# Matrix products that read their moving operand as runs of 128 columns: a decoder block in float32r on one core

## The chip, the core and the metric

The program runs on one core of a Trainium2 chip. The core has five engines with instruction queues of their own: TensorE (PE, matrix products; its weight loads have a row of their own, PEld), VectorE (DVE), ScalarE (ACT), GpSimd (POOL) and SyncE (SP, which issues most of the loads). They share an on-chip memory (SBUF) of 128 partitions; matrix products land in the accumulation memory (PSUM), in banks of 512 float32 columns.

The metric is the time of one execution on the device, in microseconds. Before the change it is 1596.77 us (median of 3 runs, 1596.67 to 1596.89).

## The reference

One layer of a decoder block over 256 tokens with 16 learned tokens put in front, width 2048. A token mixer with two branches (softmax attention with a forget gate, 8 heads; chunked gated linear attention, 4 heads) and a squared-ReLU MLP of width 8192, each after an RMS norm. All inputs are float32.

```python
def hybrid_mixer(xn, w_in, ...):
    proj = xn @ w_in                                   # 2048 x 13336
    (fq, fk, fv, ff, gq, gk, gv, gr, ga, gate_fox, gate_gla) = split(proj)
    o_fox = forgetting_attention(fq, fk, fv, ff, b_forget)
    o_gla = gated_linear_attention(gq, gk, gv, g_log)
    o_gla = head_rmsnorm(o_gla, gla_norm_g) * silu(gr)
    y = sigmoid(gate_fox) * (o_fox @ w_o_fox) + sigmoid(gate_gla) * (o_gla @ w_o_gla)
    return y @ w_out

h = concat([meta_tokens, x])
h = h + hybrid_mixer(rmsnorm(h, norm_mix_g), ...)
h = h + square(relu(rmsnorm(h, norm_mlp_g) @ w1)) @ w2
return rmsnorm(h, final_norm_g)[16:]
```

## The kernel before

Activations are kept transposed: 128 channels on the partitions, tokens along the row. Every operand of a product is held as two float32r numbers, a high part (the value cast to float32r) and a low part (what the cast left over), so that a product of two float32 matrices is made of three float32r products: high x high, high x low and low x high.

Weights come from `w_all` in chunks of 2048 input channels x 128 output channels, in the order in which they are used (`stream()`). `next_weights` loads a chunk in two halves (L118, SP), casts each to its high part on ACT (L120) and subtracts on DVE for the low part (L121). Weight halves rotate through five buffers.

The product that fills most of the program is `gemm2` (L140 ff.): for each of 16 channel blocks k it calls `mac2`, which issues two products into one bank `ps`. The first (L136) has the high weights as its stationary operand and reads 512 columns: the 256 tokens of the high part and then the 256 of the low part of the moving operand, `x[:, k]`. The second (L137) has the low weights and reads the 256 columns of the high part alone. ACT and DVE then add the two halves of the bank (`total`, L168 and L171, or `add_residual`, L858 to L860). Products over all 272 tokens (`gemm_all`, L153 to L155) come three to a block, each 272 columns wide.

The moving operands are these tiles. `x`, the normalised input, lies in the tile `x_row` (tag s1), whose row for one k has 544 words: 272 of the high part and 272 of the low part; `gemm2` reads the 512 from word 16 on. The other five come from the helper `operand` (L218 ff.): `og` (output of the linear attention, tag s2), `of` (output of the softmax attention, 8 blocks), `y` (gated sum, tag s1), `x2` (input of the MLP, tag s2) and `a` (hidden layer of the MLP, tag s1, made anew for each of four groups). It gives each k a row of 544 words too, of which 16 at each end are left unused, and hands out a view `[128, k, o, t]`: o = 0 is the high part, o = 1 the low part, t the 256 tokens. The 512 columns of one k are then one run of consecutive words, and the 256 of the high part are one run too. The rows are written by ACT (high part) and DVE (low part), mostly in `split_to` (L175, L176); `x2` by L865 and L866.

The order of the program: a first stage in which seven chunks are worked on together (L345 to L352), the four heads of linear attention, the eight of softmax attention, the gates and the two branch projections (operands `x`, `of`, `og`), the output projection (`y`), and four groups of the MLP, each 16 chunks with the operand `x2` and 16 with `a`. The last four output chunks are taken apart: their low-weight products come first (L912, 256 columns, one run) and their high-weight products then run once for each half of the tokens (L928). There the 256 columns are 128 of the high part and the same 128 tokens of the low part, so two runs of 128 with 128 words between them. Their high weights are kept in the tile `whi_last` (tag s2).

A tile framework places the instructions in the engines' queues and adds the semaphores. Nothing in the code around the change sets the order by hand, apart from the last stage.

Of the kernel before, what the change touches and what calls it, by code (L numbers as in the profile page):

```python
# [16 lines left out]
P = 128  # L17
# [48 lines left out]
def trunk(ctx: ExitStack, tc: tile.TileContext, hT, w_small, w_all, consts, w_alpha2, out):  # L66
# [3 lines left out]
    def nm(s):  # L70
        serial[0] += 1
        return f"{s}_{serial[0]}"
# [145 lines left out]
    def operand(pool, name, nk=KT, at=0, **kw):  # L218


        row = 2 * NT + 32
        t = pool.tile([P, at + nk * row], F32R, name=nm(name), **kw)
        t = t[:, at:].rearrange("p (k r) -> p k r", r=row)
        return t[:, :, 16 : 16 + 2 * NT].rearrange("p k (o t) -> p k o t", t=NT)

# [28 lines left out]
    def gain(i, k):  # L254
        return h[:, k, NA + i : NA + i + 1]
# [202 lines left out]
    def og_tile():  # L458
        if not og_box:
            og_box.append(operand(keep, "og", tag="s2"))  # L460
        return og_box[0]
# [32 lines left out]
    def gla_head(hd, sg, ready=None):  # L494
# [129 lines left out]
        def scale():  # L624
            for i in range(4):
                j = 4 * hd + i
                nc.vector.scalar_tensor_tensor(oT[:, i, :], oT[:, i, :], ggn[:, j : j + 1], rg, op0=ALU.mult,
                                               op1=ALU.mult)
                nc.vector.tensor_tensor(oT[:, i, :], oT[:, i, :], st["sg"][:, i, :], op=ALU.mult)
                split_to(og_tile()[:, j, 0, :], og_tile()[:, j, 1, :], oT[:, i, :])  # L630

# [52 lines left out]
    late = branches.enter_context(tc.tile_pool(name="late", bufs=1, reuse_waits="tile"))  # L684
    of = operand(late, "of", FOX_H, 32)
    negc = late.tile([P, FOX_H, NA], F32, name="negc")
# [18 lines left out]
    def fox_head(hd):  # L705
# [71 lines left out]
        def out_v():  # L777
            po = bank(px, "pof")
            three(po[:, 0:NT], va, pa, True, False)
            nc.tensor.matmul(po[:, P:NT], vb, pT, start=False, stop=True)  # L780
            nc.scalar.copy(of[:, hd, 0, :], po[:, 0:NT])
            nc.vector.tensor_tensor(of[:, hd, 1, :], po[:, 0:NT], of[:, hd, 0, :].bitcast(F32),
                                    op=ALU.subtract)
            nc.scalar.copy(og4[:, four], corners(po[:, 0:NT]))
# [11 lines left out]
        def fill_corners(pu, vz, pz):  # L796
            nc.tensor.matmul(pu[:, 2 * P : 3 * P], vz, pz, start=True, stop=True)
            nc.vector.tensor_tensor(og4, og4, pu[:, 2 * P : 3 * P].rearrange("p (h c q) -> p h c q", c=2, q=NM),
                                    op=ALU.add)
            hi, lo = (of[:, hd - 3 : hd + 1, o, :].rearrange("p h (c q) -> p h c q", q=P)[:, :, :, P - NM :]  # L800
                      for o in range(2))
            split_to(hi, lo, og4)

# [22 lines left out]
    for j0 in range(0, KT, 2):  # L826
# [18 lines left out]
    ht = h[:, :, NM:NA]  # L845
    x2 = operand(keep, "x2", tag="s2")

# [15 lines left out]
    for j in range(KT):  # L863
        add_residual(j, gemm2(next_weights(), y))
        nc.scalar.activation(x2[:, j, 0, :], ht[:, j, :], AF.Identity, scale=gain(1, j))  # L865
        nc.vector.scalar_tensor_tensor(x2[:, j, 1, :], ht[:, j, :], gain(1, j),  # L866
                                       x2[:, j, 0, :].bitcast(F32), op0=ALU.mult, op1=ALU.subtract)
        square_sum(j, acc2)
# [36 lines left out]

    whi = keep.tile([P, NL, KT, P], F32R, tag="s2", name="whi_last")
    ends = []
    for n in range(NL):
        j, ps = KT - NL + n, bank(pg if n < 3 else px, "ps")
        w = next_weights(whi[:, n])  # L910
        for k in range(KT):
            nc.tensor.matmul(ps[:, 0:NT], w(k)[1], a[:, k, 0, :], start=(k == 0), stop=(k == KT - 1))  # L912
        nc.vector.tensor_tensor(ht[:, j, :], ps[:, 0:NT], ht[:, j, :], op=ALU.add)
        ends.append((j, w, ps))

    def half(t0, between, within=None):
# [4 lines left out]
        for n, (j, w, ps) in enumerate(ends):  # L921
            for k in range(KT):
                if within and n == NL - 1 and k == 4:
                    ahead = within()
                elif not (within and n == NL - 1 and k > 4):
                    ahead = None
                with tc.issue_after(ahead) if ahead else nullcontext():
                    nc.tensor.matmul(ps[:, NT:], w(k)[0], a[:, k, :, tok], start=(k == 0), stop=(k == KT - 1))  # L928
            between[n]()
# [129 lines left out]
```

## Time and profile before

| | |
|---|---|
| median of 3 runs | 1596.77 us (1596.67 to 1596.89) |
| profiled execution, span from the first to the last instruction | 1595.0 us |
| PE busy | 1585.0 us, 99% |
| PEld busy | 1428.8 us, 90% |
| DVE busy | 1060.4 us, 66% |
| ACT busy | 790.8 us, 50% |
| POOL busy | 125.2 us, 8% |
| granted TensorE clock, mean | 0.998 |
| HBM over the span | 183 GB/s |

The span leaves out what lies before the first and after the last instruction; the runs are longer than it by 1596.77 - 1595.0 = 1.8 us. Matrix products are pipelined: the duration of one in a row of the profile is longer than the time from its start to the start of the next, so the cost of one is read from start to start. In the groups by line the profile leaves out numbers in names, so `x` there stands for `x` and `x2` together.

### The profile page before, as it was taken

The page shows a single profiled execution, that of the slowest core. Times are in us where ns is not written, and L with a number is a line of the kernel's source. Part 1 is how long each engine was busy: PE and PEld are TensorE (multiplying, and loading weights), DVE is VectorE, ACT ScalarE, POOL GpSimd, SP SyncE. Part 2 cuts the span into 40 slices and gives each one's busy share as a digit, 9 for nine tenths or more (in the row PEclk, how much of TensorE's full clock was granted, in tenths as well). Part 3 has the DMA queues.
Part 4 walks back from the last instruction along what each step waited for, and adds up shares of the span by engine and source line. Part 5 has one row for each costly group of instructions (what it writes and reads, how often), then busy time and mean ns, then how long its engine had stood idle before and what let it go on. Part 6 is the DMA issues. An engine that isn't in the chain of part 4 may idle for free.

```text
span 1595.0 us, 25427 instructions
## 1 busy us (share of the span) xinstructions
PE 1585.0 (99%) x9812; PEld 1428.8 (90%) x9812; DVE 1060.4 (66%) x1659; ACT 790.8 (50%) x1271; POOL 125.2 (8%) x213
## 2 busy tenths in 40 slices
PE   9999999999999999999999999999999999999997
PEld 8999999999998888888888888888888888888887
DVE  7897757676655555555777776567655776567655
ACT  6665444454455444444555544444444444444563
POOL 6011000011100000000011000000000000000022
PEclk9999999999999999999999999999999999999999
DMA  9444545454445555555555555555555555555552
GB/s 323 156 164 155 180 157 183 167 188 164 159 167 181 191 186 189 189 191 187 186 195 186 188 193 187 188 191 190 187 190 190 186 189 193 186 188 193 186 183 97
DMA packets 86602, 293.09 MB, mean 184 GB/s; under 512 B 9112, under 2 KB 16800, under 8 KB 86352
## 3 DMA queue, kind: packets, MB, share of 16 engines
q1 hardware_dynamic: 85872, 289.62, 53.8%
q8 instruction: 77, 1.26, 0.3%
q0 software_dynamic: 176, 1.12, 0.2%
q10 hardware_dynamic: 432, 0.72, 0.1%
q14 instruction: 45, 0.37, 0.1%
HBM read 289.32 MB, written 2.11 MB: 183 GB/s over the span
## 4 chain that ended last, share of the span: by engine, by line
PE 99%; DMA 0%; issue 0%; POOL 0%; ACT 0%; DVE 0%; SPq 0%; POOLq 0%; ACTq 0%
PE ps L136 51%; PE ps L137 27%; PE psa L155 5%; PE psa L154 5%; PE psa L153 5%; PE ps L345 1%; PE ps L350 1%; PE ps L928 1%; PE pa L548 1%; PE ps L912 0%; DMA raw<-w_all_dram 0%; PE po L611 0%; POOL o L976 0%; PE po L188 0%; PE ps L348 0%
## 5 line engine op out<-in xcount | busy, mean ns | idle before, releaser
L121 DVE TENSOR_TENSOR wlo<-raw,whi 128x1024 fp32r<-128x1024 f32 x522 | 641.0, 1228 | 452.8 <-ACT whi L120 449.4
L120 ACT CAST whi<-raw 128x1024 fp32r<-128x1024 f32 x522 | 548.1, 1050 | 660.0 <-PE ps L136 493.1
L136 PE MATMUL ps<-x,whi 128*128 128x512 f32 x1952 | 683.8, 393 | 0.0
L137 PE MATMUL ps<-x,wlo 128*128 128x256 f32 x1952 | 548.5, 281 | 0.0
L136 PEld LDWEIGHTS ps<-x,whi 128*128 128x128 f32 x1952 | 366.1, 188 | 80.4
L137 PEld LDWEIGHTS ps<-x,wlo 128*128 128x128 f32 x1952 | 368.3, 189 | 0.1
L136 PE MATMUL ps<-a,whi 128*128 128x512 f32 x960 | 334.3, 392 | 0.0
L137 PE MATMUL ps<-a,wlo 128*128 128x256 f32 x960 | 269.1, 281 | 0.0
L136 PEld LDWEIGHTS ps<-a,whi 128*128 128x128 f32 x960 | 179.8, 188 | 39.9
L137 PEld LDWEIGHTS ps<-a,wlo 128*128 128x128 f32 x960 | 181.1, 189 | 0.3
L153 PE MATMUL psa<-x,whi 128*128 128x272 f32 x624 | 181.2, 290 | 0.0
L155 PE MATMUL psa<-x,whi 128*128 128x272 f32 x624 | 181.1, 290 | 0.0
L154 PE MATMUL psa<-x,wlo 128*128 128x272 f32 x624 | 179.4, 288 | 0.0
L153 PEld LDWEIGHTS psa<-x,whi 128*128 128x128 f32 x624 | 118.1, 189 | 0.4
L154 PEld LDWEIGHTS psa<-x,wlo 128*128 128x128 f32 x624 | 117.4, 188 | 0.0
L155 PEld LDWEIGHTS psa<-x,whi 128*128 128x128 f32 x624 | 117.2, 188 | 0.0
L136 PE MATMUL ps<-og,whi 128*128 128x512 f32 x256 | 89.6, 392 | 0.0
L136 PE MATMUL ps<-y,whi 128*128 128x512 f32 x256 | 89.1, 392 | 0.0
L854 POOL TENSOR_TENSOR acc<-acc,hsq 128x256 f32<-128x256 f32 x26 | 28.5, 1097 | 769.2 <-ACT hsq L853 769.2
L137 PE MATMUL ps<-og,wlo 128*128 128x256 f32 x256 | 71.9, 281 | 0.0
L137 PE MATMUL ps<-y,wlo 128*128 128x256 f32 x256 | 71.8, 281 | 0.0
L171 DVE TENSOR_TENSOR evt<-ps,evb 128x256 f32<-128x256 f32 x158 | 65.9, 418 | 0.5 <-ACT evb L168 0.5
(301 smaller groups left out, 1437.0 us busy)
## 6 DMA issues: line engine op xcount, KB each, us to landing
raw<-w_all_dram SPq DMA_DIRECT2D x537, 512.0 KB, 3.6
raw<-w_all_dram SPq DMA_DIRECT2D x8, 384.0 KB, 6.6
h<-hT_dram SPq DMA_DIRECT2D x8, 275.0 KB, 6.7
negc<-fdram POOLq DMA_DIRECT2D x1, 1088.0 KB, 8.0
out_dram<-o SPq DMA_DIRECT2D x2, 512.0 KB, 2.7
raw<-w_all_dram SPq DMA_DIRECT2D x2, 256.0 KB, 3.9
room<-w_small_dram SPq DMA_DIRECT2D x1, 320.0 KB, 7.4
out_dram<-o ACTq DMA_DIRECT2D x1, 320.0 KB, 3.1
```

Of the source, the lines that this page charges most:

```text
L120: nc.scalar.copy(hi[:, k, :], r)
L121: nc.vector.tensor_tensor(lo[:, k, :], r, hi[:, k, :].bitcast(F32), op=ALU.subtract)
L136: nc.tensor.matmul(ps, hi, x, start=first, stop=False)
L137: nc.tensor.matmul(ps[:, 0:NT], lo, x[:, 0, :], start=False, stop=last)
L153: nc.tensor.matmul(ps[:, 0:NA], hi, x_hi[:, k], start=(k == 0), stop=False)
L154: nc.tensor.matmul(ps[:, 0:NA], lo, x_hi[:, k], start=False, stop=(k == KT - 1))
L155: nc.tensor.matmul(ps[:, X_LO], hi, x_lo[:, k], start=False, stop=(k == KT - 1), skip_group_check=True)
L171: nc.vector.tensor_tensor(t, ps[:, 0:NT], b, op=ALU.add)
L345: nc.tensor.matmul(ps, hi, x[:, k], start=st, stop=False)
L350: nc.tensor.matmul(ps[:, 0:NT], lo, x[:, k, 0], start=False, stop=sp)
L548: nc.tensor.matmul(dst, k[:, a], q[:, a, :], start=(a == 0), stop=(a == 1))
L854: nc.gpsimd.tensor_tensor(acc, acc, sq, op=ALU.add)
```

## The change

`operand` no longer leaves unused words between rows. A row for one k now has 512 words, split in two halves of the tokens, a = 0 and a = 1; in each half stand the 128 words of the high part and then the 128 of the low part. The view is `[128, k, o, a, t]` with t of 128. Read in the order o, a, t, the 512 columns of a product are four runs of 128 words, at words 0, 256, 128 and 384 of the row, and the 256 of the high part are two, at words 0 and 256. The order of the columns in the bank is as before. In L928 the high and low words of one half of the tokens now lie side by side, so that its 256 columns are one run.

The tile sizes stay nearly the same (`of` gets 32 words less), and the spare words serve as an offset `at` ahead of the first row: 64 for `og` and `x2`, 96 for `of` and `y`, and 96, 64, 80, 64 for the four groups of `a`. The writers address the rows as two runs of 128 (`pair`). In `fox_head` a copy and a subtraction become a call of `split_to`, which issues the same two instructions. `whi_last` begins 16 words further on. `x`, `gemm_all` and the first stage are not touched.

```diff
     def operand(pool, name, nk=KT, at=0, **kw):
-        row = 2 * NT + 32
-        t = pool.tile([P, at + nk * row], F32R, name=nm(name), **kw)
-        t = t[:, at:].rearrange("p (k r) -> p k r", r=row)
-        return t[:, :, 16 : 16 + 2 * NT].rearrange("p k (o t) -> p k o t", t=NT)
+        t = pool.tile([P, nk * (2 * NT + 32)], F32R, name=nm(name), **kw)
+        return t[:, at : at + nk * 2 * NT].rearrange("p (k a o t) -> p k o a t", a=2, o=2, t=P)
+
+    def pair(ap):
+        return ap.rearrange("p (a t) -> p a t", t=P)
...
-            og_box.append(operand(keep, "og", tag="s2"))
+            og_box.append(operand(keep, "og", at=64, tag="s2"))
...
-                split_to(og_tile()[:, j, 0, :], og_tile()[:, j, 1, :], oT[:, i, :])
+                split_to(og_tile()[:, j, 0], og_tile()[:, j, 1], pair(oT[:, i, :]))
...
-    of = operand(late, "of", FOX_H, 32)
+    of = operand(late, "of", FOX_H, 96)
...
-            nc.scalar.copy(of[:, hd, 0, :], po[:, 0:NT])
-            nc.vector.tensor_tensor(of[:, hd, 1, :], po[:, 0:NT], of[:, hd, 0, :].bitcast(F32),
-                                    op=ALU.subtract)
+            split_to(of[:, hd, 0], of[:, hd, 1], pair(po[:, 0:NT]))
...
-    y = operand(keep, "y", tag="s1")
+    y = operand(keep, "y", at=96, tag="s1")
     for j in range(KT):
-        split_to(y[:, j, 0, :], y[:, j, 1, :], yf[:, j, :])
+        split_to(y[:, j, 0], y[:, j, 1], pair(yf[:, j, :]))
...
-    x2 = operand(keep, "x2", tag="s2")
+    x2 = operand(keep, "x2", at=64, tag="s2")
...
-        nc.scalar.activation(x2[:, j, 0, :], ht[:, j, :], AF.Identity, scale=gain(1, j))
+        nc.scalar.activation(x2[:, j, 0], pair(ht[:, j, :]), AF.Identity, scale=gain(1, j))
...
-        split_to(a[:, f, 0, :], a[:, f, 1, :], s)
+        split_to(a[:, f, 0], a[:, f, 1], pair(s))
...
-        a = operand(keep, "a", tag="s1")
+        a = operand(keep, "a", at=(96, 64, 80, 64)[g], tag="s1")
...
-    whi = keep.tile([P, NL, KT, P], F32R, tag="s2", name="whi_last")
+    whi = keep.tile([P, 16 + NL * KT * P], F32R, tag="s2", name="whi_last")[:, 16:].rearrange(
+        "p (n k m) -> p n k m", k=KT, m=P)
...
-            nc.tensor.matmul(ps[:, 0:NT], w(k)[1], a[:, k, 0, :], start=(k == 0), stop=(k == KT - 1))
+            nc.tensor.matmul(ps[:, 0:NT], w(k)[1], a[:, k, 0], start=(k == 0), stop=(k == KT - 1))
...
-                    nc.tensor.matmul(ps[:, NT:], w(k)[0], a[:, k, :, tok], start=(k == 0), stop=(k == KT - 1))
+                    nc.tensor.matmul(ps[:, NT:], w(k)[0], a[:, k, :, t0 // P], start=(k == 0), stop=(k == KT - 1))
```

More of the change, by code (lines that the diff above doesn't have):

```diff
@@ L799, in fill_corners @@
                                     op=ALU.add)
-            hi, lo = (of[:, hd - 3 : hd + 1, o, :].rearrange("p h (c q) -> p h c q", q=P)[:, :, :, P - NM :]
-                      for o in range(2))
-            split_to(hi, lo, og4)
+            split_to(*(of[:, hd - 3 : hd + 1, o, :, P - NM :] for o in range(2)), og4)
         later(1, turn_v)
@@ L864, in trunk @@
         add_residual(j, gemm2(next_weights(), y))
-        nc.scalar.activation(x2[:, j, 0, :], ht[:, j, :], AF.Identity, scale=gain(1, j))
-        nc.vector.scalar_tensor_tensor(x2[:, j, 1, :], ht[:, j, :], gain(1, j),
-                                       x2[:, j, 0, :].bitcast(F32), op0=ALU.mult, op1=ALU.subtract)
+        nc.scalar.activation(x2[:, j, 0], pair(ht[:, j, :]), AF.Identity, scale=gain(1, j))
+        nc.vector.scalar_tensor_tensor(x2[:, j, 1], pair(ht[:, j, :]), gain(1, j),
+                                       x2[:, j, 0].bitcast(F32), op0=ALU.mult, op1=ALU.subtract)
         square_sum(j, acc2)
```

## The prediction

> **What bounds the kernel now.** I read the page's shares first, then the chain that ended last, then the groups by line, and last the instructions of PE in order of time.
>
> ```profile
> span 1595.0 us, 25427 instructions
> PE 1585.0 (99%) x9812; PEld 1428.8 (90%) x9812; DVE 1060.4 (66%) x1659; ACT 790.8 (50%) x1271; POOL 125.2 (8%) x213
> PEclk9999999999999999999999999999999999999999
> PE 99%; DMA 0%; issue 0%; POOL 0%; ACT 0%; DVE 0%; SPq 0%; POOLq 0%; ACTq 0%
> PE ps L136 51%; PE ps L137 27%; PE psa L155 5%; PE psa L154 5%; PE psa L153 5%; PE ps L345 1%; PE ps L350 1%; PE ps L928 1%; PE pa L548 1%; PE ps L912 0%; DMA raw<-w_all_dram 0%; PE po L611 0%; POOL o L976 0%; PE po L188 0%; PE ps L348 0%
> ...
> L136 PE MATMUL ps<-x,whi 128*128 128x512 f32 x1952 | 683.8, 393 | 0.0
> L137 PE MATMUL ps<-x,wlo 128*128 128x256 f32 x1952 | 548.5, 281 | 0.0
> L136 PE MATMUL ps<-a,whi 128*128 128x512 f32 x960 | 334.3, 392 | 0.0
> L136 PE MATMUL ps<-og,whi 128*128 128x512 f32 x256 | 89.6, 392 | 0.0
> L136 PE MATMUL ps<-y,whi 128*128 128x512 f32 x256 | 89.1, 392 | 0.0
> L136 PE MATMUL ps<-of,whi 128*128 128x512 f32 x128 | 45.1, 393 | 0.0
> ```
>
> The chain is PE for 99% of the span, and 78% of it is the two lines of `mac2`; the clock is granted in full throughout. In the groups the number behind the last bar, idle time of PE ahead of the group, is 0.0 everywhere. No semaphore holds these products up, so only their own pace counts. The mean durations (393, 281 ns) overlap; the pace is in the starts:
>
> ```profile
> 1099.76 0.39 PE L136 MATMUL ps<-x,whi 128*128 128x512 f32 x1
> 1099.99 0.28 PE L137 MATMUL ps<-x,wlo 128*128 128x256 f32 x1
> 1100.11 0.39 PE L136 MATMUL ps<-x,whi 128*128 128x512 f32 x1
> ...
> 1103.94 0.39 PE L136 MATMUL ps<-x,whi 128*128 128x512 f32 x1
> ```
>
> This is the operand `x2`. From the first to the last row shown there are 12 pairs (one L136, one L137): (1103.94 - 1099.76) / 12 = 348.3 ns a pair. The operand `a` goes at the same pace, (1002.92 - 999.79) / 9 = 347.8 ns:
>
> ```profile
> 999.79 0.39 PE L136 MATMUL ps<-a,whi 128*128 128x512 f32 x1
> ...
> 1002.92 0.39 PE L136 MATMUL ps<-a,whi 128*128 128x512 f32 x1
> ```
>
> **The change part by part.** *How many products.* The groups give 960 (`a`), 256 (`og`), 256 (`y`) and 128 (`of`) pairs; of the 1952 listed under `x`, the four MLP groups have 4 x 16 chunks x 16 blocks = 1024 with `x2`, and 928 keep the operand `x` and their one run. Changed: 2624 pairs, which now take 2624 x 348.3 ns = 914 us, 57% of the span. One nanosecond on a pair is 2.6 us. I call 0.2% (3.2 us, about what a measurement of this kernel can tell from no change) the bound of "the same"; it is 1.2 ns on a pair.
>
> *What two runs cost.* One line of the kernel before reads its 256 columns as two runs of 128 already, L928; beside it stands L912, 256 columns in one run of the same tile. The chain of the last microseconds (start, length, what) shows both with nothing between:
>
> ```profile
> 1562.51 5.68 PE ps L912 x48
> 1568.18 1.65 PE ps L928 x14
> 1569.84 0.95 PE ps L912 x8
> 1570.78 0.23 PE ps L928 x2
> 1571.02 0.94 PE ps L912 x8
> 1571.96 7.47 PE ps L928 x64
> ```
>
> One run: 5.68 / 48 = 118.3 ns. Two runs: 1.65 / 14 = 117.9 ns in the first stretch and 7.47 / 64 = 116.7 ns in the long one. A second run of 128 costs nothing that these rows show, and in the long stretch the product is 1.6 ns shorter. That is the nearest row to every product that the change touches.
>
> *L137, from one run to two* (words 0 and 256 of the row, the same step as in L928 before): 1.6 ns less by the long stretch, 0.4 by the first: 2624 x 1.6 = 4.2 us less, between 1.0 and 4.2. I take 4.2, since the long stretch is the steady one.
>
> *L136, from one run to four.* No row has four runs. With a gain for each further run it would be 3 x 1.6 = 4.8 ns, 12.6 us less. On the other side stands what a start costs: a 512-column product takes 348.3 - 118.3 = 230.0 ns, two of 256 take 236.6, so a product has some 6.6 ns that don't go with its columns (an estimate from these rows). If each of three further runs paid that, it would be 19.8 ns, 52 us more; L928 speaks against it. I take the same 1.6 ns as for two runs, once for the product: 4.2 us less.
>
> *Where the rows lie.* Rows of 544 words begin at a new place modulo 128 words with each k; rows of 512 words all begin at the same place, which `at` chooses. No row of before compares places apart from others; the 1.2 ns between the two stretches of L928, whose instruction is the same, is the size of what such things do here. I take 0; if all products of a tile sat at the better or worse end, it would be 1.2 x 2 x 2624 = 6.3 us to either side.
>
> The page "TensorE: Matmul & The Clock Gate" of the Trainium skill (section "Wait — 56ns, not 53.3ns?") has N / 2.4 GHz + 2.5 ns from start to start: 215.8 and 109.2, or 325 ns a pair, where the rows have 348.3. The trace doesn't agree, by 23 ns a pair; if the change took all of that away, an estimate by that page is 2624 x 23 ns = 60 us less, some 1536 us.
>
> *The last stage.* L928 goes from two runs to one, 128 x 1.6 = 0.2 us more; L912 from one to two, 64 x 1.6 = 0.1 less. `whi_last` moves by 16 words: 0, with both ends inside the 1.2 ns x 128 = 0.2 us of the two stretches. Together +0.1 us.
>
> *The writers.* 16 rows of `og`, 8 of `of`, 16 of `y`, 16 of `x2` and 64 of `a` are written, 120 on ACT and 120 on DVE, now as two runs:
>
> ```profile
> L176 DVE TENSOR_TENSOR a<-asq,a 128x256 fp32r<-128x256 f32 x64 | 26.6, 419 | 0.0
> L175 ACT CAST a<-asq 128x256 fp32r<-128x256 f32 x64 | 25.5, 401 | 0.0
> L121 DVE TENSOR_TENSOR wlo<-raw,whi 128x1024 fp32r<-128x1024 f32 x522 | 641.0, 1228 | 452.8 <-ACT whi L120 449.4
> L120 ACT CAST whi<-raw 128x1024 fp32r<-128x1024 f32 x522 | 548.1, 1050 | 660.0 <-PE ps L136 493.1
> ```
>
> DVE sat idle for 452.8 us ahead of L121 alone, and ACT for 660.0 ahead of L120, mostly for a free weight buffer, that is, for PE. If each write took twice as long, DVE would work 120 x 0.419 = 50 us more and ACT 48 us more, both well inside that idle time. Cost 0, covered by PE's products; were the cover gone, those 50 us would be the price. No DMA, wait or instruction is added or moved past a queue, on SP and POOL neither; the merged `split_to` issues the same two instructions.
>
> *Sum.* 1595.0 - 4.2 - 4.2 + 0.1 = 1586.7 us of span; with the 1.8 us by which the median of the runs (1596.77) exceeds it, 1588.5 us.
>
> **The rivals.** *Nothing changes.* The difference between 118.3 and 116.7 needn't be the runs: the first stretch of L928 has the same two runs and goes at 117.9. Then the pace comes from the order of loads and products, a run of 128 words is as good as one of 512, and the time stays 1596.8. For it: that first stretch. Against it: the long one, 64 products without a pause. The page "SBUF — State Buffer" of the Trainium skill (section "Specifications (TRN2)") points the same way: reads pay when they cross from one 16-byte line to the next, and runs of 128 float32 words that begin at multiples of 16 words cross as many lines as before. No run here shows that by itself.
>
> *The further runs of L136 stall the reading (slower).* L928 shows one jump inside a product of 256 columns; three jumps in 512 columns, back and forth (words 0, 256, 128, 384), may not be hidden as one is. At a quarter of a start, 1.65 ns a jump, it is 3 x 1.65 x 2624 = 13.0 us more with L137 unchanged: 1609.8. It decides from 0.4 ns a jump on (1.2 ns a pair). For it: PE waits for nothing else, so any stall shows in full. Against it: the two-run rows, where a jump costs less than nothing.
>
> *The fixed place is a bad one (slower).* The worse end above with nothing from the runs: 1596.8 + 6.3 = 1603.1. For it: 1.2 ns of difference exist for one and the same instruction. Against it: `x2` and `a` lie in different tiles and go at 348.3 and 347.8 ns.
>
> *Every further run gains.* L136 12.6 and L137 4.2 less: 1580.1; with the better end of the places too, 1573.8. For it only that the one jump seen gained.
>
> **How the numbers follow.** Forecast (1.6 ns on both products, with 1 to 2 ns either way) 0.40; every further run gains 0.12; nothing changes 0.16; the jumps stall 0.20; the fixed place is bad 0.12. Faster 0.40 + 0.12 = 0.52, the same 0.16, slower 0.20 + 0.12 = 0.32. Time 1588.5. The forecast's own range is 1583 to 1593. As both signs hold much of the chance, the range reaches down to 1575, just above the best of the gaining cases, and up to 1612, which takes in the stall at its price and leaves out dearer jumps (at half a start, 1622.8); outside lie 0.08 below and 0.12 above.
>
> **What would show each step.** `x` stays as it is, so its 928 pairs should still go at 348.3 ns and the three lines of `gemm_all` as before: they are the measure within the same profile. Pairs of `x2`, `a`, `og`, `y` and `of` should go at 345.1 ns (348.3 - 3.2), all alike; if the tiles differ, the place counts and not the runs. If the 512-column start-to-start grows and the 256 one doesn't, it is the jumps. L912 and L928 should change places, 116.7 and 118.3 ns. The idle time of PE ahead of L136 should stay 0.0; if it isn't, a writer or the order of the instructions has changed, and the prediction is wrong by a cause it calls free. It would be wrong above all if the pace of a pair went by something that neither L912 nor L928 shows, since 57% of the span rests on a difference of 1.6 ns between them.

## The result and the profile after

The changed kernel takes 1606.88 us (median of 4 runs, 1606.86 to 1607.11), against 1596.72 us (1596.59 to 1596.89) for the kernel before on the same chip: a ratio of 1.0063 [1.005, 1.0077], so it is slower by 10.2 us. The profiled execution spans 1605.4 us, 10.4 more than before. The granted clock is 0.999.

The page of the changed kernel shows the span, the busy time of the engines, the chain that ended last, and the groups by line (busy time and mean of one, then idle time ahead):

```profile
span 1605.4 us, 25427 instructions
PE 1594.9 (99%) x9812; PEld 1429.5 (89%) x9812; DVE 1060.8 (66%) x1659; ACT 791.1 (49%) x1271; POOL 126.6 (8%) x213
PE 98%; DMA 0%; issue 0%; POOL 0%; SPq 0%; ACT 0%; DVE 0%; POOLq 0%; ACTq 0%
...
L121 DVE TENSOR_TENSOR wlo<-raw,whi 128x1024 fp32r<-128x1024 f32 x522 | 641.1, 1228 | 462.7 <-ACT whi L120 461.9
L136 PE MATMUL ps<-x,whi 128*128 128x512 f32 x1952 | 688.9, 396 | 0.0
L137 PE MATMUL ps<-x,wlo 128*128 128x256 f32 x1952 | 549.2, 281 | 0.0
```

The same number of instructions, still no idle time ahead of L136, DVE and ACT as busy as before, and DVE with 10 us more idle time ahead of L121 (462.7 for 452.8). All of the 10 us is on PE, 1594.9 for 1585.0, with nothing in between: the products themselves go more slowly. Which of them, the rows of PE in order of time tell (start, length; the first and the last L136 of a stretch of pairs, in the order `x`, `x2` for group 0, `a` of groups 0, 1 and 2):

```profile
548.38 0.39 PE L136 MATMUL ps<-x,whi 128*128 128x512 f32 x1
...
570.33 0.39 PE L136 MATMUL ps<-x,whi 128*128 128x512 f32 x1
...
1076.92 0.40 PE L136 MATMUL ps<-x,whi 128*128 128x512 f32 x1
...
1110.48 0.40 PE L136 MATMUL ps<-x,whi 128*128 128x512 f32 x1
...
987.34 0.39 PE L136 MATMUL ps<-a,whi 128*128 128x512 f32 x1
...
1020.83 0.39 PE L136 MATMUL ps<-a,whi 128*128 128x512 f32 x1
...
1167.36 0.40 PE L136 MATMUL ps<-a,whi 128*128 128x512 f32 x1
...
1200.92 0.40 PE L136 MATMUL ps<-a,whi 128*128 128x512 f32 x1
...
1348.00 0.39 PE L136 MATMUL ps<-a,whi 128*128 128x512 f32 x1
...
1381.28 0.39 PE L136 MATMUL ps<-a,whi 128*128 128x512 f32 x1
```

Between the rows of a stretch lie 63, 95, 96, 95 and 96 pairs, so a pair takes 348.4 ns with `x`, which the change doesn't touch, 33.56 / 95 = 353.3 with `x2`, and 348.9, 353.3 and 346.7 with `a` in groups 0, 1 and 2. Before, each of these tiles went at 348.3. The tiles have the same four runs and differ only in where their rows begin. Added up tile by tile, against 348.3 ns:

| tile | begins at (words modulo 128) | pairs | ns a pair | us more |
|---|---|---|---|---|
| `x2` | 80 | 1024 | 353.3 | 5.1 |
| `og` | 80 | 256 | 353.3 | 1.3 |
| `y` | 112 | 256 | 353.3 | 1.3 |
| `of` | 80 | 128 | 351.1 and 353.3 by turns | 0.5 |
| `a` group 0 | 112 | 256 | 353.1 and 351.9 in the first two chunks, then 348.9 | 0.3 |
| `a` group 1 | 80 | 256 | 353.3 | 1.3 |
| `a` group 2 | 96 | 256 | 353.0, 351.0, then 346.7 | -0.3 |
| `a` group 3 | 80 | 192 | 353.3 | 1.0 |

The sum is 10.5 us, the 10.4 by which the span grew. The places are the addresses that the framework gave out: the tiles with tag s1 and s2 begin at 16 modulo 128 and `of`'s at 112, to which `at` is added; every weight tile, high and low, begins at 32 (`whi_last` too, which stood at 16 before). In the kernel before, rows of 544 words turned through 32, 64, 96 and 0 from one k to the next, in all tiles alike.

In the last stage the chain (start, length, what) has the two lines that the prediction started from, L912 now L909 and L928 now L925:

```profile
1572.98 5.66 PE ps L909 x48
...
1582.41 7.54 PE ps L925 x64
```

L909 now reads two runs, at 5.66 / 48 = 117.9 ns, and L925 one, at 7.54 / 64 = 117.8. The 1.6 ns that lay between them have not changed sides; they are gone.

### The profile page after: what moved, and what is told of

It is laid out like the page before. It is cut to its first block, busy times and chain, and to the rows that moved or that the text cites. A ratio compares the mean times of both kernels' runs of the same rounds, so it can differ in the third digit from the quotient of the medians.

```text
span 1605.4 us, 25427 instructions
## 1 busy us (share of the span) xinstructions
PE 1594.9 (99%) x9812; PEld 1429.5 (89%) x9812; DVE 1060.8 (66%) x1659; ACT 791.1 (49%) x1271; POOL 126.6 (8%) x213
## 4 chain that ended last, share of the span: by engine, by line
PE 98%; DMA 0%; issue 0%; POOL 0%; SPq 0%; ACT 0%; DVE 0%; POOLq 0%; ACTq 0%
PE ps L136 51%; PE ps L137 26%; PE psa L155 5%; PE psa L154 5%; PE psa L153 5%; PE ps L345 1%; PE ps L925 1%; PE ps L350 1%; PE pa L548 1%; PE ps L909 0%; DMA raw<-w_all_dram 0%; PE po L611 0%; POOL o L973 0%; PE po L188 0%; PE psa L655 0%
## 5 line engine op out<-in xcount | busy, mean ns | idle before, releaser
L121 DVE TENSOR_TENSOR wlo<-raw,whi 128x1024 fp32r<-128x1024 f32 x522 | 641.1, 1228 | 462.7 <-ACT whi L120 461.9
L136 PE MATMUL ps<-x,whi 128*128 128x512 f32 x1952 | 688.9, 396 | 0.0
L137 PE MATMUL ps<-x,wlo 128*128 128x256 f32 x1952 | 549.2, 281 | 0.0
L136 PEld LDWEIGHTS ps<-x,whi 128*128 128x128 f32 x1952 | 366.8, 188 | 84.7
L137 PEld LDWEIGHTS ps<-x,wlo 128*128 128x128 f32 x1952 | 367.7, 188 | 0.1
L136 PE MATMUL ps<-a,whi 128*128 128x512 f32 x960 | 336.5, 396 | 0.0
L137 PE MATMUL ps<-a,wlo 128*128 128x256 f32 x960 | 268.4, 280 | 0.0
L136 PEld LDWEIGHTS ps<-a,whi 128*128 128x128 f32 x960 | 180.2, 188 | 42.7
L137 PEld LDWEIGHTS ps<-a,wlo 128*128 128x128 f32 x960 | 180.3, 188 | 0.4
L136 PE MATMUL ps<-og,whi 128*128 128x512 f32 x256 | 90.8, 397 | 0.0
L136 PE MATMUL ps<-y,whi 128*128 128x512 f32 x256 | 90.4, 396 | 0.0
L137 PE MATMUL ps<-y,wlo 128*128 128x256 f32 x256 | 72.1, 282 | 0.0
L137 PE MATMUL ps<-og,wlo 128*128 128x256 f32 x256 | 72.0, 281 | 0.0
```

Source lines behind the costliest of these rows:

```text
L121: nc.vector.tensor_tensor(lo[:, k, :], r, hi[:, k, :].bitcast(F32), op=ALU.subtract)
L136: nc.tensor.matmul(ps, hi, x, start=first, stop=False)
L137: nc.tensor.matmul(ps[:, 0:NT], lo, x[:, 0, :], start=False, stop=last)
```

## The experiments

Three theories stood at the start. The place: a pair's pace goes by where the rows begin. The jumps: each step from one run to the next costs something. The lines: a run that doesn't begin at a multiple of 32 words touches one line of 128 bytes more, so that many runs at bad places cost much. Paces are from start to start of L136, over some 95 pairs as above, or over one chunk of 16 with the step to the next chunk. The 346.5 of the expectations is the pace that 96 pairs give as 346.7. "Place" is the first word of a row modulo 128.

### All rows at multiples of 32 words

Four runs as in the change; `of` begins at 64, all others at 96.

```diff
-            og_box.append(operand(keep, "og", at=64, tag="s2"))
+            og_box.append(operand(keep, "og", at=80, tag="s2"))
-    of = operand(late, "of", FOX_H, 96)
+    of = operand(late, "of", FOX_H, 80)
-    y = operand(keep, "y", at=96, tag="s1")
+    y = operand(keep, "y", at=80, tag="s1")
-    x2 = operand(keep, "x2", at=64, tag="s2")
+    x2 = operand(keep, "x2", at=80, tag="s2")
-        a = operand(keep, "a", at=(96, 64, 80, 64)[g], tag="s1")
+        a = operand(keep, "a", at=(80, 80, 80, 80)[g], tag="s1")
```

> The changed kernel with every offset chosen so that the rows begin at a multiple of 32 words (128 bytes): at = 80 for og, of, y, x2 and all four groups of a; four runs of 128 as in the changed kernel. Theory of lines (a product pays for each 128-byte line that it touches, and a run that begins 16 words into a line touches one line more): a run of 128 words touches 4 lines instead of 5, a pair (512 and 256 columns) 24 instead of 30; pairs go at 348.3 ns or at the 346.5 of the one aligned group of the changed kernel, and the time is 1592 to 1597 us. Theory of jumps (each further run of a product costs, wherever it lies): nothing changes, 353.3 ns a pair and about 1607 us (a little over, as the group that went at 349 loses its luck).

1603.65 us, 1.0042 [1.0027, 1.0057]. Rows of PE, `x2` in group 1 and in group 2:

```profile
1075.76 0.40 PE L136 MATMUL ps<-x,whi 128*128 128x512 f32 x1
...
1109.32 0.40 PE L136 MATMUL ps<-x,whi 128*128 128x512 f32 x1
...
1254.70 0.39 PE L136 MATMUL ps<-x,whi 128*128 128x512 f32 x1
...
1287.98 0.39 PE L136 MATMUL ps<-x,whi 128*128 128x512 f32 x1
```

33.56 / 95 = 353.3 and 33.28 / 96 = 346.7 ns: the same tile, at the same place, read by the same lines, has two paces. Behind its first two chunks `a` went at 353.3 in groups 0 and 2 and at 346.7 in 1 and 3, and `y` at 346.7; `og` went at 353.2, `of`, at 64, at 351.0. This was a miss for every theory: aligned rows are not all fast, and a place does not settle a pace alone.

### Other places, four runs

```diff
-            og_box.append(operand(keep, "og", at=64, tag="s2"))
+            og_box.append(operand(keep, "og", at=72, tag="s2"))
-    y = operand(keep, "y", at=96, tag="s1")
+    y = operand(keep, "y", at=68, tag="s1")
-        a = operand(keep, "a", at=(96, 64, 80, 64)[g], tag="s1")
+        a = operand(keep, "a", at=(16, 48, 80, 112)[g], tag="s1")
```

The four groups of `a` now begin at 32, 64, 96 and 0, `og` at 88, `y` at 84.

> The changed kernel with other offsets, one place for each tile, so that one profile compares places: first word modulo 32 is 24 for og, 20 for y, 16 for of and x2 (as in the changed kernel), and 0 for the four groups of a, which begin at 32, 64, 96 and 0 modulo 128. Theory of lines of 128 bytes: og, y, of and x2 all at 353.3 ns a pair, whatever the remainder is; all groups of a at 346.5 to 348.3; about 1604 us. If the lines were of 64 bytes, og and y would be slower than x2, since they alone begin inside such a line. Theory of jumps: 353.3 everywhere, 1607 us or more. Theory of a fixed place modulo 128: the four groups of a differ from one another.

1605.08 us (one run). `a` in group 0 and in group 1:

```profile
986.43 0.39 PE L136 MATMUL ps<-a,whi 128*128 128x512 f32 x1
...
1019.71 0.39 PE L136 MATMUL ps<-a,whi 128*128 128x512 f32 x1
...
1165.88 0.40 PE L136 MATMUL ps<-a,whi 128*128 128x512 f32 x1
...
1199.24 0.39 PE L136 MATMUL ps<-a,whi 128*128 128x512 f32 x1
```

346.7 ns at place 32 (96 pairs) and 33.36 / 95 = 351.2 at 64; group 2 (96) went as group 0, both behind two slower chunks (353.0 and 351.1), and group 3 (0) as group 1. So 32 and 96 are alike, 64 and 0 are alike, and the two kinds differ by 4.5 ns although all four are multiples of 32 words. `y` went at 350.0, `og` at 352.5 and 353.3 by turns. The place counts, modulo 64; lines of 32 words don't explain it.

### One run, rows of 544, moved by 16 words

```diff
-        return t[:, :, 16 : 16 + 2 * NT].rearrange("p k (o t) -> p k o t", t=NT)
+        return t[:, :, 0 : 2 * NT].rearrange("p k (o t) -> p k o t", t=NT)
```

> The kernel before (one run of 512, one of 256, rows of 544 words), with the rows of og, of, y, x2 and a begun 16 words earlier, so that they start 16 words into a 128-byte line. Theory of lines: 17 lines instead of 16 and 9 instead of 8, two more for a pair where the changed kernel had six more for 5.0 ns; so 348.3 + 1.7 = 350.0 ns a pair, 1596.7 + 4.4 = 1601 us. Theory of jumps: no further run, no change, 1596.7 us. Theory that the start inside a line costs a product a fixed sum whatever the runs: 353.3 ns a pair and 1609 us.

1601.52 us, 1.0028 [1.0017, 1.004]. `x2` in group 2:

```profile
1253.43 0.39 PE L136 MATMUL ps<-x,whi 128*128 128x512 f32 x1
...
1287.03 0.39 PE L136 MATMUL ps<-x,whi 128*128 128x512 f32 x1
```

33.60 / 96 = 350.0 ns, in every tile alike: 1.7 ns a pair more, with one run and 16 words of shift. The number is near what the lines gave, but by the run above and the next two they don't hold; here rows turn through four places that lie 16 words off those of before.

### Eight runs of 64 words

```diff
-        return t[:, at : at + nk * 2 * NT].rearrange("p (k a o t) -> p k o a t", a=2, o=2, t=P)
+        return t[:, at : at + nk * 2 * NT].rearrange("p (k a o t) -> p k o a t", a=4, o=2, t=C)
...
-            og_box.append(operand(keep, "og", at=64, tag="s2"))
+            og_box.append(operand(keep, "og", at=80, tag="s2"))
-    of = operand(late, "of", FOX_H, 96)
+    of = operand(late, "of", FOX_H, 80)
-    y = operand(keep, "y", at=96, tag="s1")
+    y = operand(keep, "y", at=80, tag="s1")
-    x2 = operand(keep, "x2", at=64, tag="s2")
+    x2 = operand(keep, "x2", at=80, tag="s2")
-        a = operand(keep, "a", at=(96, 64, 80, 64)[g], tag="s1")
+        a = operand(keep, "a", at=(80, 64, 80, 64)[g], tag="s1")
```

The writers' `pair` and two other lines, one that writes and one that reads, follow the rows in quarters.

> The changed kernel with rows in quarters of the tokens: the 512 columns are eight runs of 64 words, the 256 are four. og, of, y, x2 and the groups 0 and 2 of a begin at a multiple of 32 words, groups 1 and 3 of a 16 words further. Theory of lines: an aligned run of 64 touches 2 lines, so the aligned tiles touch no more than one run does and go at 346.5 to 348.3 ns a pair; a shifted run touches 3, 36 lines a pair instead of 24, at 5.0 ns for six 348.3 + 10 = 358.3 ns in groups 1 and 3; 1596.7 + 448 x 10 ns = 1601 us. Theory of jumps, at 5.0 ns for the four further runs of the changed kernel: ten further runs cost 12.5 ns, 360.8 ns in every tile, 1596.7 + 2624 x 12.5 ns = 1629.5 us.

1604.95 us (one run). `a` in group 1, which begins at 80:

```profile
1166.92 0.40 PE L136 MATMUL ps<-a,whi 128*128 128x512 f32 x1
...
1200.49 0.40 PE L136 MATMUL ps<-a,whi 128*128 128x512 f32 x1
```

33.57 / 95 = 353.4 ns with eight runs, as the change has with four at the same place; `a` in group 2, at 96, went at 346.7 behind its first two chunks. Twice as many runs and jumps cost nothing, at a good place or a bad one. Jumps and lines are out.

### The change's places with one run

Rows of 512 words, the same `at`, the same shift of `whi_last`, but the high part in one piece and then the low part: one run for L136 and for L137, two for the last stage as before.

```diff
-        row = 2 * NT + 32
-        t = pool.tile([P, at + nk * row], F32R, name=nm(name), **kw)
-        t = t[:, at:].rearrange("p (k r) -> p k r", r=row)
-        return t[:, :, 16 : 16 + 2 * NT].rearrange("p k (o t) -> p k o t", t=NT)
+        t = pool.tile([P, nk * (2 * NT + 32)], F32R, name=nm(name), **kw)
+        return t[:, at : at + nk * 2 * NT].rearrange("p (k o t) -> p k o t", o=2, t=NT)
```

> The kernel before with one run of 512 columns and one of 256, but with rows of 512 words and the offsets of the changed kernel, so that every row of og, of and x2 begins at word 80 modulo 128, those of y at 112 and those of a at 112, 80, 96, 80. Theory of the fixed place (the pace of a pair goes by the place modulo 128 words at which the rows begin, and rows of 512 words hold all products of a tile at one place): the same paces as in the changed kernel without its runs, 353.3 ns for og, x2, y and the groups 1 and 3 of a, 349 to 353 for group 0, 346.5 for group 2; 1606.9 us. Theory of runs, or of runs together with lines: 348.3 to 350.0 ns a pair, 1597 to 1601 us.

1606.76 us, 1.0066 [1.0048, 1.0084]. `x2` in group 0, and from the chain the long stretch of the last stage's high-weight products:

```profile
1076.49 0.40 PE L136 MATMUL ps<-x,whi 128*128 128x512 f32 x1
...
1110.06 0.40 PE L136 MATMUL ps<-x,whi 128*128 128x512 f32 x1
```

```profile
1581.98 7.54 PE ps L926 x64
```

353.4 ns with one run. Every tile's pace is that of the changed kernel, chunk by chunk, and so is the time: the whole loss comes without any of the runs that the change makes. And L926, which here has two runs, takes 117.8 ns as L925 does with one: the 116.7 of before did not belong to two runs.

### Four runs with the rows of before

```diff
-        t = pool.tile([P, nk * (2 * NT + 32)], F32R, name=nm(name), **kw)
-        return t[:, at : at + nk * 2 * NT].rearrange("p (k a o t) -> p k o a t", a=2, o=2, t=P)
+        row = 2 * NT + 32
+        t = pool.tile([P, at + nk * row], F32R, name=nm(name), **kw)
+        t = t[:, at:].rearrange("p (k r) -> p k r", r=row)[:, :, 16 : 16 + 2 * NT]
+        return t.rearrange("p k (a o t) -> p k o a t", a=2, o=2)
```

The `at` are those of before.

> The changed kernel with its four runs of 128, but with rows of 544 words again, so that the place moves by 32 words with each k as in the kernel before. Theory of the fixed place: 348.3 ns a pair in every tile, 1596.8 us. Theory of runs: 353.3 ns, 1607 us or more.

1596.94 us, 1.0002 [0.9992, 1.0012]. `x2` in group 0, and from the chain the last stage's two lines:

```profile
1072.59 0.39 PE L136 MATMUL ps<-x,whi 128*128 128x512 f32 x1
...
1106.03 0.39 PE L136 MATMUL ps<-x,whi 128*128 128x512 f32 x1
```

```profile
1563.20 5.68 PE ps L911 x48
...
1572.67 7.57 PE ps L927 x64
```

33.44 / 96 = 348.3 ns, in every tile; in the last stage 118.3 ns with two runs (5.68 / 48) and 118.3 with one (7.57 / 64). The runs alone cost nothing and gain nothing; with the run before this one, the two halves of the change are told apart.

### The weights 16 words further on

The changed kernel with one tile ahead of the weights made 16 words longer, so that all weight tiles but `whi_last` begin at 48 instead of 32 and the operands stay; `of` keeps its place by a smaller `at`.

```diff
-    rb = keep.tile([P, NA], F32, tag="rb", name="rb")
+    rb = keep.tile([P, NA + 16], F32, tag="rb", name="rb")[:, 0:NA]
-    of = operand(late, "of", FOX_H, 96)
+    of = operand(late, "of", FOX_H, 80)
```

> The changed kernel with all weight tiles 16 words further on in the memory (place 48 modulo 128 instead of 32), the moving operands where they were. If the pace goes by the place of the moving operand against that of the weights, counted modulo 64 words (0: 346.5 or 353.3; 32: 351.1; 48: 353.3; 16: 349 or 353.3): og, x2 and the groups 1 and 3 of a go from 353.3 to 351.1 ns, group 2 from 346.5 to 353.3, y and group 0 to 346.5 or 353.3, and the operand x, which is not touched, from 348.3 to the 349.9 that shifted rows showed; 1603 to 1606 us. If it goes by the place of the moving operand alone, all paces stay as in the changed kernel and so does the 1606.9 us.

1605.2 us (one run). `x2` in group 0 and `a` in group 2, which both lie where the change puts them:

```profile
1076.12 0.40 PE L136 MATMUL ps<-x,whi 128*128 128x512 f32 x1
...
1109.48 0.39 PE L136 MATMUL ps<-x,whi 128*128 128x512 f32 x1
...
1345.91 0.40 PE L136 MATMUL ps<-a,whi 128*128 128x512 f32 x1
...
1379.47 0.40 PE L136 MATMUL ps<-a,whi 128*128 128x512 f32 x1
```

`x2` at 80 went from 353.3 to 33.36 / 95 = 351.2, `a` at 96 from 346.7 to 353.3, and `x`, whose rows turn, from 348.3 to 349.9, the pace that 16 words of shift gave in the third experiment. The others went as expected too: `og` at 351.0, `y` at 353.4, `a` in groups 1 and 3 at 351.1, and in group 0 at 346.7 behind its first two chunks. Of what these pairs read, only the weights moved; but the raw weights, and every tile placed behind them, moved by the same 16 words. ACT, DVE and POOL, which use those tiles, are not needed for the slow pace: in the changed kernel 13 pairs of `a` in group 1 ran while none of the three was at work, and took 353.3 ns like the rest (the DMA queues were at work in every one of them). So the distance between the operand's rows and the weights, modulo 64 words, told the paces beforehand.

It does not settle them alone. In the last stage L925 reads `a` at 80 and its weights from `whi_last`, and neither moved:

```profile
1580.67 7.26 PE ps L925 x64
```

That is 113.4 ns a product, where the changed kernel had 117.8. Whether the products ahead of this stretch make the difference, or another tile that moved, no run tells.

The page "TensorE: Matmul & The Clock Gate" of the Trainium skill (section "Part 2: What happens when you issue a matmul") says that the two have separate read ports: "Loading the next tile's weights doesn't steal SBUF read bandwidth from the running matmul." The trace doesn't bear out that the weights leave a running product alone: with the weights moved, and the tiles behind them, its pace changed by -2.2 to +6.6 ns a pair. What the two reads share, no row shows.

### Only some tiles at a fixed place, one run

Rows of 512 words with one run for `y` and `a` alone, then `a` alone, then `a` and `x2`, all at 96, and last `x2` at 32 with `a` at 96; everything else as before the change. The core of it, for `a`:

```diff
+        if at >= 16 and nk == KT:
+            t = pool.tile([P, nk * row], F32R, name=nm(name), **kw)
+            return t[:, at : at + nk * 2 * NT].rearrange("p (k o t) -> p k o t", o=2, t=NT)
...
-        a = operand(keep, "a", tag="s1")
+        a = operand(keep, "a", at=80, tag="s1")
```

> The kernel before with rows of 512 words that begin at word 96 modulo 128 for y and a alone, one run each; x2, og and of keep rows of 544. At word 96 two paces were seen, 346.5 and 353.3 ns. If a group of a starts in the slow one and leaves it after its first chunk, as the group at that place did in the changed kernel: 15 of 16 chunks at 346.5, so 1216 pairs x 1.8 ns = 2.2 us less, 1594.6 us, the first that would be faster than the kernel before. If it starts in the fast one and turns slow, 1216 x 5.0 ns = 6.1 us more, 1602.9 us.

`y` and `a`: 1596.44 us, 0.9998 [0.9989, 1.0008]. `a` went at 346.7 and `y` at 353.3; with 960 pairs gaining 1.65 ns (1.6 us) and 256 losing 5.0 (1.3 us), they nearly cancel. The time lies between the two cases of the expectation, since neither had the tiles part ways.

> The kernel before with rows of 512 words that begin at word 96 modulo 128 (64 words from the place of the weights) for a alone, one run each; og, of, y and x2 keep rows of 544. Theory of the place against the weights, with the two paces seen there: a starts and stays at 346.5 ns as it did with y fixed too, 960 x 1.8 = 1.7 us less, 1595.0 us; the rest as in the kernel before. If a turns to the slow pace, 960 x 5.0 = 4.8 us more, 1601.5 us.

`a` alone: 1595.18 us, 0.9989 [0.998, 0.9998], as expected. All groups of `a` went at 346.7.

> As the last, and x2 too in rows of 512 words that begin at word 96 modulo 128. The two sums after the first chunk of x2 disturb the order of products once. If x2 keeps or finds the fast pace, another 1024 x 1.8 = 1.8 us less, 1593.2 us; if it stays in the slow one, which four-run rows at this place did in three groups of four, 3 x 256 x 5.0 = 3.8 us more for those and 1 to 2 us for the groups of a behind them, about 1599 us.

`a` and `x2`: 1599.4 us, 1.0017 [1.0008, 1.0026]. `x2` in group 1 and in group 2:

```profile
1072.85 0.39 PE L136 MATMUL ps<-x,whi 128*128 128x512 f32 x1
...
1106.13 0.39 PE L136 MATMUL ps<-x,whi 128*128 128x512 f32 x1
...
1148.07 0.62 PE L136 MATMUL ps<-a,whi 128*128 128x512 f32 x2
1148.53 0.40 PE L137 MATMUL ps<-a,wlo 128*128 128x256 f32 x2
...
1252.30 0.40 PE L136 MATMUL ps<-x,whi 128*128 128x512 f32 x1
...
1285.86 0.40 PE L136 MATMUL ps<-x,whi 128*128 128x512 f32 x1
```

346.7 ns and then 33.56 / 95 = 353.3. Groups 0 and 2 of `x2` went one way and 1 and 3 the other; of `a`, groups 0 and 2 at 346.7, 1 and 3 at 353.3. The two rows in the middle are where it turned: in each group of `a` the framework once lets two chunks overlap, so that two L136 come in a row and then two L137. The kernel before has the same rows at the same point and stayed at 348.3. Ahead of such a point the pace was one of the two, behind it the other. `x2` turned in group 0 alone, at the two sum products that come behind its first chunk; in the other groups it kept the pace in which the `a` ahead of it had ended.

Such a point doesn't turn the pace each time. With `a` alone fixed, and with `y` and `a`, the weights and the place of `a` are the same as here, all four groups have the same rows, and `a` went at 346.7 ahead of them and behind. With `a` alone, in group 1:

```profile
1147.52 0.63 PE L136 MATMUL ps<-a,whi 128*128 128x512 f32 x2
```

And with all rows at multiples of 32 words, `a` in group 0 stayed at 353.3.

> As the last with x2 at word 32 modulo 128, the very place of the weights, and a at 96. If only the distance modulo 64 words counts, the same two paces for x2 as at word 96, 346.5 or 353.3 ns, and the same time as the last kernel. If the distance counts modulo 128, x2 has one pace of its own in all groups.

`x2` at 32: 1599.78 us, 1.0018 [1.0009, 1.0027], tile for tile as with `x2` at 96. Again 32 and 96 are one place.

### Only the low weights 16 words further on

To see which of the two weight loads counts, a tile of 16 words was put between the high and the low weights: high at 32, low at 48. `x2` at 96, `og` at 80, `y` at 64, `a` at 96 and 80 in turn.

```diff
+        if c0 == 0 and k0 == 0:
+            nc.gpsimd.memset(wp.tile([P, 16], F32, tag="gap", name=nm("gap"), bufs=1), 0.0)
```

> The kernel before with the low weights alone 16 words further on (place 48, the high weights stay at 32) and rows of 512 words at one place for each tile: x2 and the groups 0 and 2 of a at 96, og and the groups 1 and 3 of a at 80, y at 64. Which load does a product meet? While the 512 columns of L136 are read, the low weights for L137 are loaded, and the other way round. If a product is held up by the load that runs beside it: at 80, L136 is 32 words from the low weights (230.6 ns from start to start, as the other runs had it at that distance) and L137 48 from the high ones (118.3), 348.9 ns a pair; at 96, 235.0 + 115.2 = 350.2. If it is its own weights that count: at 80, 235.0 + 120.5 = 355.5 ns; at 96, 232.0 + 118.3 = 350.3. If the weights' place does not count at all, 353.3 at 80.

1599.09 us (one run). `x2` in group 0 and `a` in group 1, at 80:

```profile
1073.26 0.39 PE L136 MATMUL ps<-x,whi 128*128 128x512 f32 x1
...
1106.54 0.39 PE L136 MATMUL ps<-x,whi 128*128 128x512 f32 x1
...
1162.42 0.39 PE L136 MATMUL ps<-a,whi 128*128 128x512 f32 x1
...
1195.99 0.39 PE L136 MATMUL ps<-a,whi 128*128 128x512 f32 x1
```

346.7 and 353.4 ns. Both theories of the loads miss: `x2` stayed fast, and `og`, at 80 like this group of `a`, went at 350.0 to 350.4. `y`, at 64, went at 346.7 behind its first two chunks. That the high weights alone count, as in the expectation's last case, would fit `x2` and `a`, but not `og` (350.2 for 353.3) or `y` (346.7 for 351.1). At 96 the pace didn't turn in this run: `x2` and groups 0 and 2 of `a` went at 346.7 over the same points of disturbance. As `a` kept its pace there without the gap too, when it alone was fixed, it is not shown that the gap does it. Which load counts stays open.

### A version that keeps the fast pace

The low weights as in the last run, and all five operands in rows of 512 words at 96: once with one run, on the kernel before, and once with the change's four runs; the lines are those of the second, against the changed kernel.

```diff
+        if c0 == 0 and k0 == 0:
+            nc.gpsimd.memset(wp.tile([P, 16], F32, tag="gap", name=nm("gap"), bufs=1), 0.0)
-            og_box.append(operand(keep, "og", at=64, tag="s2"))
+            og_box.append(operand(keep, "og", at=80, tag="s2"))
-    y = operand(keep, "y", at=96, tag="s1")
+    y = operand(keep, "y", at=80, tag="s1")
-    x2 = operand(keep, "x2", at=64, tag="s2")
+    x2 = operand(keep, "x2", at=80, tag="s2")
-        a = operand(keep, "a", at=(96, 64, 80, 64)[g], tag="s1")
+        a = operand(keep, "a", at=(80, 80, 80, 80)[g], tag="s1")
```

> The kernel before with the low weights 16 words further on (place 48, the high ones at 32) and all five operands in rows of 512 words that begin at word 96 modulo 128, one run each. If the single pace that x2 and a showed there, 346.7 ns, holds for every tile and isn't left at a disturbance: 2624 x 1.6 = 4.2 us less than before, 1592.5 us, or some 1593 with x a little slower, as that run had it. If one of the smaller tiles (og, of, y) goes at 353.3 there: 640 x 5.0 = 3.2 us of it is lost, 1595 to 1596 us.

> The changed kernel, four runs of 128 and all, with these places: low weights at 48, all operands at 96. If runs cost nothing and the place is all: the same 346.7 ns a pair as with one run, and the same time, 1592.5 to 1593 us, faster than the kernel before. If the runs cost something that the slow places had hidden, it is slower than the one-run kernel of the same places.

One run: 1594.7 us (11 runs, 1594.1 to 1595.13), 0.9986 [0.9977, 0.9995]. Four runs: 1594.99 us (11 runs, 1594.46 to 1595.86), 0.9988 [0.9979, 0.9997]. But for the first two chunks of `of`, the pairs of the five tiles took 346.65 ns in both, so runs are free at the fast pace too, and both kernels are faster than the two of this case, by 0.14% and 0.12% than the one before. Neither turned at any of the six points of disturbance. The first and the last row of 45 products of `gemm_all` in one chunk, and `x2` in group 0, of the one-run version:

```profile
169.82 0.29 PE L153 MATMUL psa<-x,whi 128*128 128x272 f32 x1
...
175.52 0.29 PE L153 MATMUL psa<-x,whi 128*128 128x272 f32 x1
...
1072.27 0.39 PE L136 MATMUL ps<-x,whi 128*128 128x512 f32 x1
...
1105.55 0.39 PE L136 MATMUL ps<-x,whi 128*128 128x512 f32 x1
```

and the same 45 products of the kernel before:

```profile
168.91 0.28 PE L153 MATMUL psa<-x,whi 128*128 128x272 f32 x1
...
174.56 0.29 PE L153 MATMUL psa<-x,whi 128*128 128x272 f32 x1
```

The pairs gain 4.2 us (2624 x 1.65 ns, less the first of `of`). But with the low weights shifted `gemm_all` takes 5.70 - 5.65 = 0.05 us more in these 15 blocks; by the starts of all its 624 blocks it is 1.6 us, `x` loses 0.3 us, and the rest of the program 0.4. That leaves 1.9 us; the profiled executions differ by 1.8 (1595.0 to 1593.2), the medians by 2.2 (1596.9 to 1594.7). The expected time, 1592.5, left these costs out.

### The paces together

All by distance from the weights to the row's first word, modulo 64 words, both weight tiles at one place:

| distance | ns a pair | seen in |
|---|---|---|
| 0 | 346.7 or 353.3 | rows at 96 or 32 with weights at 32; weights at 48 with rows at 112 |
| 16 | 348.9 or 353.3 | the change: `a` group 0, `y` |
| 32 | 351.1 | rows at 0 and 64; weights at 48 with rows at 80 |
| 48 | 353.3 | the change: `x2`, `og`, `a` groups 1 and 3; weights at 48 with rows at 96 |
| 52 | 350.0 | `y` at 84 |
| 56 | 352.5 and 353.3 by turns | `og` at 88 |
| turning 0, 32 | 348.3 | before; four runs with rows of 544 |
| turning 16, 48 | 349.9 to 350.0 | moved by 16 words; `x` with the weights moved |

## Why the prediction was wrong

The sign was wrong: 1588.5 us was forecast, with faster the likeliest, and 1606.88 came, by the case that it called "the fixed place is a bad one" and priced at 1603.1. The stated range, 1575 to 1612, holds the time.

*What two runs cost* is the step that failed first, and with it the sign. It took the 1.6 ns between L912 (118.3) and L928 (116.7) for the price of a run. The kernel with the change's places and one run has two runs in that line as before, at 117.8 ns, and with four runs and the rows of before the two lines, which have changed roles, both take 118.3. With the weights moved, one run took 113.4. So neither term of -4.2 us for L137 and L136 exists. The warning was in the rows: the first stretch of L928, the same instruction, went at 117.9, and the long stretch was preferred as the steady one.

*Where the rows lie* is the term that was mis-sized. It was set to 0 with 6.3 us to either side; it is the whole result, +10.4 us of span, as the one-run kernel at the change's places shows. The bound had been drawn from two stretches of one line, 1.2 ns a product and 2.4 a pair, while the places differ by up to 6.7 ns a pair (346.65 to 353.3). The argument against the rival was void: `x2` and `a` going at 348.3 and 347.8 said nothing of places, because in the kernel before the rows of both turn through the same four. A pace that is alike in all tiles is what an average over places looks like; the text had noted that rows of 544 begin at a new place with each k and did not draw the conclusion that 348.3 was such an average. It held that no row of before compares places, but the starts of before do, once they are averaged by k: behind the 500th us, over 112 pairs for each place, `x` took 345.8 ns with rows at 96, 348.3 at 32 and at 0, and 350.8 at 64. (`y` had nearly the same values at other places: 346.1 at 32, 347.9 at 96, 348.4 at 64, 350.8 at 0. So there too the place has a part and doesn't settle the pace alone.)

*Nothing changes* was right on the runs, and the four runs with the rows of before show it (1.0002), but the time still changed. *The further runs stall* and *every further run gains* both fall with it: eight runs, four and one go alike.

*The test named beforehand* was half good. "If the tiles differ, the place counts and not the runs" gave the answer from the rows of the changed kernel alone. "If the 512-column start-to-start grows and the 256 one doesn't, it is the jumps" would have misled: in the groups L136 does grow, from a mean of 393 to 396 ns, while L137 stays at 281, yet with one run at the same places the same two means appear.

*The rest held.* No idle time came ahead of L136, the writers' longer rows stayed under the idle time of DVE and ACT, and `x` and the chain kept their shape. The last stage's +0.1 us can't be told from nothing: L909 and L925 now take 117.9 and 117.8 ns, not 116.7 and 118.3.

**What stays open.** Why one and the same place has two paces, and when a disturbance in the order of the products makes it turn; the runs show that it can, in kernels with one run and with four, and that it doesn't each time. Why the distance to the weights counts: that the operand's rows get in the way of a weight load is only argued, the run with the low weights moved answered for neither load, and in the last stage the pace changed with the distance left as it was. And the paces of turning rows are only near the mean of their fixed places (348.9 for 0 and 32 with the faster of the two paces, against 348.3 measured), so the table is a record of this kernel and no law.

## What to carry to other kernels

Where PE never waits, a change of layout is to be read for the first word of each row against the weights' first word as well as for its runs: here 16 words of difference were worth up to 6.7 ns in 350, and cutting a product's columns into two, four or eight runs was worth nothing. A pace that is the same everywhere is no sign that the place doesn't count if all tiles turn through the same places; padding that makes rows turn gave a middle pace here, and a fixed place a better or a worse one that had to be measured. Two parts of a change that come together, a new order and new addresses, are told apart by two kernels, each with one of them.

## What was not expected of the hardware

A float32r pair of 512 and 256 columns changed its pace by up to 2% (346.65 to 353.3 ns) with the distance, modulo 64 words, between the rows that it reads and the tiles that its weights are loaded from; moving the weights, and the tiles behind them, by 16 words did it (351.2 for 353.3, and 353.3 for 346.7). At distance 0 there are two paces, and a pair of products out of the usual order can turn the one into the other for hundreds of products, in some kernels and not in others; with the low weights 16 words further on and all rows at 96 none turned (346.65 ns throughout). Reading 512 columns as one, four or eight runs made no difference at any place tried.
